# One chunk recurrence of a hybrid decoder layer: both head pairs of a batch in step, products in one array shape

## The chip, the core and the metric

The kernel runs on one core of a Trainium2 chip. The metric is the device time of one execution in microseconds (us). Engines are named as in the profile: PE is TensorE's matmul row and PEld its weight loads, DVE is VectorE, ACT ScalarE, POOL GpSimd, SP SyncE.

## What is computed

One layer over 256 tokens of width 2048: a wide input projection feeds three token mixers (Mamba-2 SSD, S5, RWKV-7), whose outputs are gated, merged, projected and normalised. The change touches the RWKV-7 mixer alone, 16 heads of 64:

```
def rwkv7_recurrence(r, w, k, v, a, bvec):
    b, s, h, n = r.shape

    def step(state, inp):
        r_t, w_t, k_t, v_t, a_t, b_t = inp
        sa = jnp.einsum('bhvk,bhk->bhv', state, a_t)
        state = (state * w_t[:, :, None, :] + sa[..., None] * b_t[:, :, None, :]
                 + v_t[..., None] * k_t[:, :, None, :])
        return state, jnp.einsum('bhvk,bhk->bhv', state, r_t)
...
    y = rwkv7_recurrence(rh, heads(decay), kh, vh, -kk, kk * heads(a))
    mean = jnp.mean(y, -1, keepdims=True)
    var = jnp.mean(jnp.square(y - mean), -1, keepdims=True)
    y = ((y - mean) * lax.rsqrt(var + RWKV_LNX_EPS)).reshape(b, s, RWKV_WIDTH) * lnx_w + lnx_b
```

The kernel does not step token by token. It cuts the 256 tokens into 4 chunks of 64 and writes each chunk as a few 64 by 64 products, with a triangular inverse for the part inside the chunk; only the state S goes from chunk to chunk.

## The kernel before

**Projections.** Most of the work is `proj`: a tile of 128 output columns, 16 blocks of the inner dimension, and for each block three matmuls of 128x128 by 128x256 in a reduced float32 format (L381 to L383), since weights and activations are split into a high and a low part. The weights come by DMA in half tiles (L367); ACT makes the high part (L369), DVE the low one (L371). Every half tile passes through a ring of four buffers.

**RWKV stage.** The 16 heads are 8 head pairs `hp` (a pair fills the 128 partitions, head 0 in rows 0 to 63, head 1 in rows 64 to 127); two pairs form a batch `b`, `i` is the pair in it. The list `PROG` gives the order of emission: `F` is the front of a batch, `T` the inverse of its diagonal blocks, `C` its chunk loop, the other entries are projections placed between. The framework's scheduler, which simulates a timeline, then sets each engine's order of instructions; each engine works through its own in order. So the small matmuls of the recurrence stand scattered between projections in PE's order, at most some twenty projections apart.

- `rwkv_prep` makes the operands of a head pair: `pv` (L585, V by token, four chunks of one head after the other), `pt` (L591, transposes of the stack of b and k), `pa` (L603, the products inside a chunk). `XS` holds the operands of the state product, `SVA` a stack of state and V for each head, `bkT` the transposed stacks, `MTr` the masked products with r.
- `rwkv_tinv` inverts the 32 by 32 diagonal blocks on DVE (L629, L630), brings them back by DMA into `TTf`, and adds the blocks beside the diagonal by three small products `py` (L647, L651, L655), 32 by 32.
- `rwkv_chunks` is the loop over four chunks, and in it over the two pairs of the batch. For each it multiplies XS by SVA (L675), copies the result to X (ACT, L677), multiplies by the inverse TTf (L680), copies it into SVA (ACT, L683), multiplies by bkT for the state's increment (L687), decays and adds the state (ACT L693, DVE L694; L690 in the first chunk), and forms the output: SVA by MTr (L697) plus, from the second chunk on, the old state by XS (L699). ACT copies the output to XS (L700). The next chunk begins with two ACT copies of S into SVA (L671).

These small products are in full float32, which PE does in two passes, each with its own weight load. L675 (but for the first chunk), L687 and L697 work on 128 rows and 64 columns of the array; L680, L699, L585 and the first chunk's L675 on 64 rows and 64 columns, one quadrant for each head.

Of the kernel before, what the change touches and what calls it, by code (L numbers as in the profile page):

```python
# [95 lines left out]
def pack(x, w_in, ssd_conv_w, ssd_conv_b, ssd_dt_bias, ssd_a_log, ssd_d, ssd_norm_w,  # L96
# [124 lines left out]
        # rings with one tile more than is alive, so that the low parts of a split take their sources' places  # L221
# [79 lines left out]
def setup(g):  # L301
# [3 lines left out]
    with tc.high_priority(), tc.tile_pool(name="xp", bufs=1) as xp:  # L305
# [11 lines left out]
        # step sizes of the SSD heads, kept in DRAM until their stage  # L317
# [28 lines left out]
    class Half:  # L346
        """[128, 16, 128] in two tiles of 8."""
# [59 lines left out]
CL = 64  # L407
# [3 lines left out]
def rwkv_setup(g):  # L411
# [10 lines left out]
    g.half = rp.tile([128, 2], F32, name="half")        # 0.5 | -0.5*exp(-0.5)  # L422
# [53 lines left out]
def rwkv_front(g, b):  # L476
# [13 lines left out]
    bt.XS, bt.bkT, bt.MTr, bt.SVA, bt.bon, bt.W4 = [], [], [], [], [], []  # L490
    bt.Aoff = rp.tile([128, 2, NCH, 32], F32, name=f"Aoff{b}", tag=f"Aoff{b % 2}", bufs=1)
    bt.TTf = rp.tile([128, 2, NCH, 64], F32, name=f"TTf{b}", tag=f"TTf{b % 2}", bufs=1)
    nc.gpsimd.memset(bt.TTf, 0.0)
    # blocks: [hp 2][c 4][h 2][half 2][s 32][t 32]
# [20 lines left out]
def rwkv_prep(g, bt, b, i, K, R, V, rh):  # L515
# [3 lines left out]
    # LoRA: decay logits and a logits  # L519
# [23 lines left out]
    W4 = rp.tile([128, NCH], F32, name=f"W4{hp}", tag="W4", bufs=4)  # L543
    nc.scalar.activation(W4, EE[:, :, CL], AF.Copy)
# [7 lines left out]
    # stack slots: 0 = head 0 (rows 0-63 A~, 64-127 Aak), 1 = head 1 (rows 0-63 Aak, 64-127 A~), 2 = r~  # L552
# [5 lines left out]
    # k2 = k*(1 + (a-1)*k_a); a = 0.5 + 0.5*tha  # L558
# [6 lines left out]
    BK = rp.tile([128, NCH, 3, CL], F32, name=f"BK{hp}", tag="BK", bufs=1)    # b, k, b  # L565
# [3 lines left out]
    # bonus = (sum r*k2*r_k) * v  # L569
# [6 lines left out]
    # token-major V, less its mean over the head (the recurrence is linear in V, so its outputs are centred), and (b, k) stacks  # L576
    SVA = rp.tile([128, 2, NCH, 64], F32, name=f"SVA{hp}", tag=f"SVA{b % 2}", bufs=2)
    bkT = rp.tile([128, 2, NCH, 64], F32, name=f"bkT{hp}", tag=f"bkT{b % 2}", bufs=2)
    pv = g.pp.tile([128, 2, NCH, 64], F32, name=f"pv{hp}", tag="s", bufs=2)
    idn = g.c("ident")  # L580
    for h in range(2):
        r = slice(64 * h, 64 * h + 64)
        o = slice(64 - 64 * h, 128 - 64 * h)
        for c in range(NCH):
            nc.tensor.matmul(pv[o, h, c, :], lhsT=V[r, CL * c:CL * c + CL], rhs=g.c("cen")[r, r], start=True, stop=True)  # L585
        nc.scalar.activation(SVA[o, h, :, :], pv[o, h, :, :], AF.Copy)
    for h in range(2):
        r = slice(64 * h, 64 * h + 64)
        pt = g.pp.tile([128, NCH, 64], F32, name=f"pt{hp}_{h}", tag="s", bufs=2)
        for c in range(NCH):  # L590
            nc.tensor.transpose(pt[:, c, :], BK[r, c, h:h + 2, :].rearrange("p a t -> p (a t)"), idn[r, r])  # L591
        nc.scalar.activation(bkT[:, h], pt, AF.Copy)
    # A stage
# [716 lines left out]
```

## Time and profile before

| | us |
|---|---|
| three runs | 1373.37, 1374.41, 1375.53 |
| median | 1374.41 |
| span of the profiled execution, first to last instruction | 1372.4 |
| PE busy in it | 1353.5 |
| DVE busy | 964.9 |
| ACT busy | 829.1 |

The profile holds the span of its execution and no other time of it; the median of the runs is 2.0 us above that span. In the views, a timeline row gives the start of an instruction and its duration; matmuls are pipelined, so that a row's duration reaches into the next rows, and the distance from start to start tells how fast PE goes. Rows of equal instructions that follow each other are merged, "x4" being four passes.

### The profile page before, as it was taken

The numbers are of one execution on the slowest core, as the hardware profiler recorded it, in microseconds if no ns is written. First come the engines' busy times: TensorE is split into PE (matmuls) and PEld (weight loads), VectorE is DVE, ScalarE is ACT, GpSimd is POOL, SyncE is SP. The second block draws the span as 40 slices with busy tenths as digits, with TensorE's granted clock in tenths as the row PEclk, the third lists the DMA queues.
The fourth block names the chain that finished last, engine by engine and source line by source line (L and its number), as shares of the span: only waits on it lengthen the run. The fifth ranks groups of instructions, "written<-read, shape, count | busy, mean of one in ns | idle before, by whom it ended". The sixth has DMA issues, their size and how long they took to land.

```text
span 1372.4 us, 28474 instructions
## 1 busy us (share of the span) xinstructions
PE 1353.5 (99%) x11436; PEld 1268.5 (92%) x11436; DVE 964.9 (70%) x1765; ACT 829.1 (60%) x1507; POOL 7.4 (1%) x54
## 2 busy tenths in 40 slices
PE   7999999999999999999999999999999999999996
PEld 7999989988999899899999999999999999999885
DVE  5658876455866765579999966799776665547755
ACT  5657565567555556887668877676645544444431
POOL 0000000000000000000000000000000000000000
PEclk9999999999999999999999999999999999999998
DMA  8545554433454345456555555555655556668751
GB/s 293 167 130 161 170 156 150 138 110 120 142 152 141 126 147 154 124 159 194 164 173 170 178 172 173 155 168 180 188 176 173 174 184 202 197 209 253 245 179 62
DMA packets 96661, 230.12 MB, mean 168 GB/s; under 512 B 26545, under 2 KB 41233, under 8 KB 96529
## 3 DMA queue, kind: packets, MB, share of 16 engines
q1 hardware_dynamic: 95936, 227.42, 53.9%
q8 instruction: 90, 1.47, 0.4%
q10 hardware_dynamic: 592, 0.89, 0.2%
q14 instruction: 43, 0.34, 0.1%
HBM read 224.00 MB, written 3.21 MB: 166 GB/s over the span
## 4 chain that ended last, share of the span: by engine, by line
PE 97%; ACT 1%; DMA 1%; DVE 1%; issue 0%; SPq 0%; DVEq 0%
PE ps_g L381 7%; PE ps_g L382 7%; PE ps_g L383 7%; PE ps_x L381 5%; PE ps_x L382 5%; PE ps_x L383 5%; PE br L1156 5%; PE br L1155 4%; PE br L1157 4%; PE po L1259 2%; PE po L1257 2%; PE po L1258 2%; PE ps_za L382 2%; PE ps_za L381 2%; PE ps_za L383 2%; PE ps_r L381 1%
## 5 line engine op out<-in xcount | busy, mean ns | idle before, releaser
L381 PE MATMUL ps_g<-xhi,hi_g 128*128 128x256 f32 x768 | 218.5, 284 | 0.0
L382 PE MATMUL ps_g<-xlo,hi_g 128*128 128x256 f32 x768 | 217.9, 284 | 0.0
L383 PE MATMUL ps_g<-xhi,lo_g 128*128 128x256 f32 x768 | 216.9, 282 | 0.0
L371 DVE TENSOR_TENSOR lo_g<-raw_g,hi_g 128x1024 fp32r<-128x1024 f32 x96 | 117.5, 1224 | 74.2 <-ACT hi_g L369 69.6
L369 ACT ACTIVATE hi_g<-raw_g 128x1024 fp32r<-128x1024 f32 x96 | 101.5, 1058 | 110.9 <-PE ps_g L382 81.8
L381 PE MATMUL ps_x<-xhi,hi_x 128*128 128x256 f32 x512 | 147.3, 288 | 0.0
L382 PE MATMUL ps_x<-xlo,hi_x 128*128 128x256 f32 x512 | 147.0, 287 | 0.0
L383 PE MATMUL ps_x<-xhi,lo_x 128*128 128x256 f32 x512 | 146.8, 287 | 0.0
L382 PEld LDWEIGHTS ps_g<-xlo,hi_g 128*128 128x128 f32 x768 | 144.6, 188 | 1.9 <-issue 0.8
L381 PEld LDWEIGHTS ps_g<-xhi,hi_g 128*128 128x128 f32 x768 | 144.6, 188 | 1.7
L383 PEld LDWEIGHTS ps_g<-xhi,lo_g 128*128 128x128 f32 x768 | 144.6, 188 | 0.9 <-issue 0.4
L369 ACT ACTIVATE hi_b<-raw_b 128x1024 fp32r<-128x1024 f32 x64 | 67.8, 1059 | 74.3 <-PE br L1156 42.9
L371 DVE TENSOR_TENSOR lo_x<-raw_x,hi_x 128x1024 fp32r<-128x1024 f32 x64 | 78.2, 1223 | 39.1 <-ACT hi_x L369 38.7
L381 PEld LDWEIGHTS ps_x<-xhi,hi_x 128*128 128x128 f32 x512 | 97.2, 190 | 2.3 <-issue 1.6
L382 PEld LDWEIGHTS ps_x<-xlo,hi_x 128*128 128x128 f32 x512 | 97.2, 190 | 2.1 <-issue 1.1
L383 PEld LDWEIGHTS ps_x<-xhi,lo_x 128*128 128x128 f32 x512 | 97.1, 190 | 1.6 <-issue 1.1
L369 ACT ACTIVATE hi_x<-raw_x 128x1024 fp32r<-128x1024 f32 x64 | 67.5, 1054 | 48.7 <-PE ps_x L382 25.1
L371 DVE TENSOR_TENSOR lo_b<-raw_b,hi_b 128x1024 fp32r<-128x1024 f32 x64 | 78.2, 1222 | 24.5 <-ACT hi_b L369 22.8
L382 PE MATMUL ps_za<-xlo,hi_za 128*128 128x256 f32 x256 | 73.1, 285 | 0.0
L381 PE MATMUL ps_za<-xhi,hi_za 128*128 128x256 f32 x256 | 73.0, 285 | 0.0
L383 PE MATMUL ps_za<-xhi,lo_za 128*128 128x256 f32 x256 | 72.6, 284 | 0.0
L1156 PE MATMUL br<-yh0l,hi_b 128*128 128x256 f32 x256 | 72.3, 283 | 0.0
(441 smaller groups left out, 4075.5 us busy)
## 6 DMA issues: line engine op xcount, KB each, us to landing
raw_g<-in_wt SPq DMA_DIRECT2D x96, 512.0 KB, 3.8
raw_x<-in_wt SPq DMA_DIRECT2D x64, 512.0 KB, 3.7
raw_za<-in_wt SPq DMA_DIRECT2D x32, 512.0 KB, 3.7
raw_b<-in_wba SPq DMA_DIRECT2D x32, 512.0 KB, 4.1
raw_wo<-in_wout SPq DMA_DIRECT2D x32, 512.0 KB, 4.7
raw_k<-in_wt SPq DMA_DIRECT2D x16, 512.0 KB, 3.8
raw_r<-in_wt SPq DMA_DIRECT2D x16, 512.0 KB, 3.7
raw_v<-in_wt SPq DMA_DIRECT2D x16, 512.0 KB, 3.6
```

Of the source, the lines that this page charges most:

```text
L369: nc.scalar.activation(hi, raw, AF.Copy)
L371: nc.vector.tensor_tensor(lo, raw, hi.bitcast(F32), ALU.subtract)
L381: nc.tensor.matmul(ps, lhsT=hi.k(k), rhs=g.xhi[:, k, :], start=(k == 0), stop=False)
L382: nc.tensor.matmul(ps, lhsT=hi.k(k), rhs=g.xlo[:, k, :], start=False, stop=False)
L383: nc.tensor.matmul(ps, lhsT=lo.k(k), rhs=g.xhi[:, k, :], start=False, stop=(k == NK - 1))
L1155: nc.tensor.matmul(ps, lhsT=hi.k(k0 + k), rhs=h, start=(k == 0), stop=False)
L1156: nc.tensor.matmul(ps, lhsT=hi.k(k0 + k), rhs=l, start=False, stop=False)
L1157: nc.tensor.matmul(ps, lhsT=lo.k(k0 + k), rhs=h, start=False, stop=(k == n - 1))
L1257: nc.tensor.matmul(po, lhsT=m[0][:, t], rhs=hi.k512(k), start=f0, stop=False)
L1258: nc.tensor.matmul(po, lhsT=m[0][:, t], rhs=lo.k512(k), start=False, stop=False)
L1259: nc.tensor.matmul(po, lhsT=m[1][:, t], rhs=hi.k512(k), start=False, stop=l0)
```

## The change

- In the chunk loop both pairs of a batch are done in step: one PSUM tile `ps` for both, one X copy, one copy into SVA for each head. The order of the matmuls is pair by pair with the two heads alternating.
- All five products of the loop use all 128 rows and 64 columns. Where an operand has only 64 rows of content, the others are zeros: `TTf` gets an axis for the head, the state is kept in `g.Sz` (two buffers, zeros in the other head's half), SVA's first chunk is zeroed.
- The state is written by DVE straight into SVA of the next chunk (add L710, multiply by the decay L711, for each head), and copied by ACT into `Sz` (L713). The fused operations L693, L694 and the copies L671 go.
- The output is gathered in a PSUM tile of its own, `chy`, for all four chunks, and copied once at the end; `ps` has two buffers instead of three.
- `pv` uses all 128 rows too, and in `pv`, `pt`, `pa` and the first product of `py` the loops run chunk by chunk with the heads alternating.

```
-            ps = g.pr.tile([128, 4, 64], F32, name=f"ch{hp}_{c}", tag="r", bufs=3)
+        ps = g.pr.tile([128, 3, 2, 64], F32, name=f"ch{b}_{c}", tag="r", bufs=2)
+        for i, h in IH:
+            nc.tensor.matmul(ps[rows[h], 0, i, :], lhsT=bt.XS[i][:, h, cs], rhs=SVA[:, i, h, c, :], start=True, stop=True)
+        X = rp.tile([128, 2, 64], F32, name=f"X{b}_{c}", tag="X", bufs=2)
+        nc.scalar.activation(X, ps[:, 0], AF.Copy)
+        for i, h in IH:
+            nc.tensor.matmul(ps[rows[h], 1, i, :], lhsT=bt.TTf[:, h, i, c, :], rhs=X[:, i, :], start=True, stop=True)
+        for h in range(2):
+            nc.scalar.activation(SVA[rows[h], :, h, c, :], ps[rows[h], 1], AF.Copy)
+        last = c == NCH - 1
+        if not last:
+            for i, h in IH:
+                nc.tensor.matmul(ps[rows[h], 2, i, :], lhsT=bt.bkT[i][:, h, c, :], rhs=SVA[:, i, h, c, :], start=True, stop=True)
...
+                nc.tensor.matmul(py[rows[h], i, cs], lhsT=SVA[:, i, h, c, :], rhs=bt.MTr[i][:, h, c, :], start=True, stop=(c == 0))
             for h in range(2):
...
+                if c > 0:
+                    nc.tensor.matmul(py[rows[h], i, cs], lhsT=Sz[:, i, h, :], rhs=bt.XS[i][:, 2, cs], start=False, stop=True)
+        if not last:
+            w = bt.W4[:, :, c:c + 1].to_broadcast([128, 2, 64])
+            Sn = g.Sz[c % 2]
...
+                    nc.vector.tensor_tensor(t, ps[r, 2], Sz[r, :, h, :], ALU.add)
+                    nc.vector.tensor_tensor(o, t, w[r], ALU.mult)
             for h in range(2):
...
+                nc.scalar.activation(Sn[rows[h], :, h, :], SVA[rows[h], :, h, c + 1, :], AF.Copy)
+            Sz = Sn
```

In `rwkv_prep`:

```
+    for c in range(NCH):
+        for h in range(2):
+            o = slice(64 - 64 * h, 128 - 64 * h)
+            nc.tensor.matmul(pv[o, h, c, :], lhsT=V[:, CL * c:CL * c + CL], rhs=g.c("cen")[:, 64 * h:64 * h + 64], start=True, stop=True)
...
+    pas = [g.pp.tile([128, NCH, 2, CL], F32, name=f"pa{hp}_{h}", tag="s", bufs=2) for h in range(2)]
+    for c in range(NCH):
+        for h in range(2):
+            r = slice(64 * h, 64 * h + 64)
+            rhs = XS[r, h:3:2 - h, CL * c:CL * c + CL]
+            nc.tensor.matmul(pas[h][:, c, :, :], lhsT=BK[r, c, h:h + 2, :].rearrange("p a t -> p (a t)"), rhs=rhs, start=True, stop=True)
```

What became of the order on PE, in batch 0. Before, at the outputs of the second chunk of pair 1 and the third of pair 0 (`ch1_1`, `ch0_2`), between the projections of a tile:

```order
L381 MATMUL ps_g2_5_3446<-xhi_69,hi_g2_5_1_3442 128x256
L697 MATMUL ch1_1_2083<-MTr1_877,SVA1_852 64x64
L699 MATMUL ch1_1_2083<-XS1_834,S1_0_2056 64x64
L697 MATMUL ch1_1_2083<-MTr1_877,SVA1_852 64x64
L699 MATMUL ch1_1_2083<-XS1_834,S1_0_2056 64x64
L697 MATMUL ch0_2_2105<-MTr0_649,SVA0_624 64x64
L699 MATMUL ch0_2_2105<-XS0_606,S0_1_2074 64x64
L697 MATMUL ch0_2_2105<-MTr0_649,SVA0_624 64x64
L699 MATMUL ch0_2_2105<-XS0_606,S0_1_2074 64x64
L675 MATMUL ch1_2_2127<-SVA1_852,XS1_834 64x64 x2
L382 MATMUL ps_g2_5_3446<-xlo_70,hi_g2_5_1_3442 128x256
```

And after, at the second chunk of batch 0 (L693 is now the product with bkT, L696 the one with MTr, L699 the one with the state):

```order
L382 MATMUL ps_g2_4_3246<-xlo_70,hi_g2_4_0_3236 128x256
L696 MATMUL chy0_2033<-MTr0_655,SVA0_448 64x64
L693 MATMUL ch0_1_2059<-SVA0_448,bkT0_631 64x64 x2
L693 MATMUL ch0_1_2059<-SVA0_448,bkT1_857 64x64 x2
L696 MATMUL chy0_2033<-MTr0_655,SVA0_448 64x64
L699 MATMUL chy0_2033<-XS0_613,Sz0_231 64x64 x2
L696 MATMUL chy0_2033<-MTr1_881,SVA0_448 64x64 x2
L699 MATMUL chy0_2033<-XS1_839,Sz0_231 64x64 x2
L383 MATMUL ps_g2_4_3246<-xhi_69,lo_g2_4_0_3238 128x256
```

The twelve matmuls of a chunk's end stand together in one shape (128 rows by 64 columns, all of them), where before the shape turned with every matmul.

On PE after the change, at `pt` of pair 0 and `pa` of pair 1 (the second number in `pa1_0` is the head); before, all of `pt` and `pa` stand in groups of one head:

```order
L601 MATMUL pt0_0_643<-cst_168,BK0_622 128x64 x4
L382 MATMUL ps_k2_918<-xlo_70,hi_k2_0_908 128x256
L383 MATMUL ps_k2_918<-xhi_69,lo_k2_0_910 128x256
L381 MATMUL ps_k2_918<-xhi_69,hi_k2_1_914 128x256
L382 MATMUL ps_k2_918<-xlo_70,hi_k2_1_914 128x256
L601 MATMUL pt0_1_644<-cst_168,BK0_622 128x64 x4
```

```order
L612 MATMUL pa1_0_882<-XS1_839,BK1_848 128x128 x2
L612 MATMUL pa1_1_883<-XS1_839,BK1_848 128x128 x2
L612 MATMUL pa1_0_882<-XS1_839,BK1_848 128x128
L612 MATMUL pa1_1_883<-XS1_839,BK1_848 128x128
L612 MATMUL pa1_0_882<-XS1_839,BK1_848 128x128
L612 MATMUL pa1_1_883<-XS1_839,BK1_848 128x128
```

The scheduler has put some of the alternating source back into groups of one head, and left some alternating.

On DVE after the change, at the state update of the second chunk of batch 0 (`St` is the sum, L371 are splits of projection weights, L641 and L642 belong to the inverse of batch 1):

```order
L641 TENSOR_TENSOR Pm1_2170<-TT1_2169,AT1_2168 128x256
L371 TENSOR_TENSOR lo_z4_1_3306<-raw_z4_1_3302,hi_z4_1_3304 128x1024
L642 TENSOR_REDUCE TT1_2169<-Pm1_2170 128x8
L710 TENSOR_TENSOR St0_1_2084<-ch0_1_2059,Sz0_231 64x128 x2
L711 TENSOR_TENSOR SVA0_448<-St0_1_2084,W40_447 64x2x64 x2
L371 TENSOR_TENSOR lo_g2_5_0_3364<-raw_g2_5_0_3360,hi_g2_5_0_3362 128x1024
```

Four operations stand where before there was one L694 for each pair, at two places.

## Rows read from the trace of the kernel before

**Rows 1.** The page, part 1: busy time, share of span, instructions.

```profile
PE 1353.5 (99%) x11436; PEld 1268.5 (92%) x11436; DVE 964.9 (70%) x1765; ACT 829.1 (60%) x1507; POOL 7.4 (1%) x54
```

**Rows 2.** All waits of PE: us in total, times, longest.

```profile
PE ps_dt L320 <- ACT wd L315: 7.0, 1, 7.0
PE ps_lora L383 <- DVE lo_lora L371: 0.4, 1, 0.4
```

**Rows 3.** Timeline of PE, 216.49 to 217.77: start, duration, engine, line, tiles.

```profile
216.49 0.28 PE L381 MATMUL ps_g<-xhi,hi_g 128*128 128x256 f32 x1
216.61 0.28 PE L382 MATMUL ps_g<-xlo,hi_g 128*128 128x256 f32 x1
216.82 0.33 PE L680 MATMUL ch<-X,TTf 64*64 64x64 f32 x2
217.08 0.39 PE L383 MATMUL ps_g<-xhi,lo_g 128*128 128x256 f32 x1
217.30 0.28 PE L381 MATMUL ps_g<-xhi,hi_g 128*128 128x256 f32 x1
217.51 0.34 PE L687 MATMUL ch<-SVA,bkT 128*64 128x64 f32 x4
217.77 0.39 PE L382 MATMUL ps_g<-xlo,hi_g 128*128 128x256 f32 x1
```

**Rows 4.** Timeline of PE at 198 us, first passes of two matmuls, different heads.

```profile
197.99 0.27 PE L680 MATMUL ch<-X,TTf 64*64 64x64 f32 x1
198.00 0.27 PE L675 MATMUL ch<-SVA,XS 64*64 64x64 f32 x1
```

**Rows 5.** Timeline of PE: eight passes of two heads in either shape.

```profile
228.68 0.45 PE L680 MATMUL ch<-X,TTf 64*64 64x64 f32 x8
229.06 0.39 PE L383 MATMUL ps_z<-xhi,lo_z 128*128 128x256 f32 x1
...
231.98 0.45 PE L687 MATMUL ch<-SVA,bkT 128*64 128x64 f32 x8
232.36 0.39 PE L382 MATMUL ps_g<-xlo,hi_g 128*128 128x256 f32 x1
```

**Rows 6.** Timeline of PE, 459.02 to 460.82: two shapes taking turns, eight times.

```profile
459.02 0.33 PE L697 MATMUL ch<-MTr,SVA 128*64 128x64 f32 x2
459.28 0.32 PE L699 MATMUL ch<-XS,S 64*64 64x64 f32 x2
...
460.82 0.33 PE L699 MATMUL ch<-XS,S 64*64 64x64 f32 x2
```

**Rows 7.** Timeline of PE: one head's `pv`, `py` of two heads, one head's `pa`.

```profile
117.86 0.68 PE L585 MATMUL pv<-cst,V 64*64 64x64 f32 x8
118.47 0.39 PE L383 MATMUL ps_z<-xhi,lo_z 128*128 128x256 f32 x1
...
176.16 0.69 PE L647 MATMUL py<-cst,TTf 32*32 32x32 f32 x16
176.78 0.33 PE L675 MATMUL ch<-SVA,XS 64*64 64x64 f32 x4
...
128.14 1.16 PE L603 MATMUL pa<-XS,BK 64*128 64x128 f32 x8
```

**Rows 8.** Window 462.00 to 465.20: busy PE, PEld, DVE, ACT, POOL; granted clock; DMA.

```profile
462.00:465.20 3.20, 3.20 (x17) 3.20 (x16) 2.40 (x6) 0.00 (x0) 0.00 (x0) 0.50 0.50 169
```

**Rows 9.** Groups by line: busy us, mean ns; idle before, releaser.

```profile
L369 ACT ACTIVATE hi_g<-raw_g 128x1024 fp32r<-128x1024 f32 x96 | 101.5, 1058 | 110.9 <-PE ps_g L382 81.8 <-issue 11.3 <-PE ps_u L382 5.5
L371 DVE TENSOR_TENSOR lo_g<-raw_g,hi_g 128x1024 fp32r<-128x1024 f32 x96 | 117.5, 1224 | 74.2 <-ACT hi_g L369 69.6 <-PE s5pk L1064 4.2
L694 DVE SCALAR_TENSOR_TENSOR S<-ch,W,SW 128x64 f32<-128x64 f32 x16 | 4.2, 274 | 12.1 <-PE ch L687 10.8 <-ACT SVA L683 1.2
```

**Rows 10.** Weight loads of L697: four in the timeline; all, with the mean ns.

```profile
205.13 0.20 PEld L697 LDWEIGHTS ch<-MTr,SVA 128*64 128x64 f32 x4
...
L697 PEld LDWEIGHTS ch<-MTr,SVA 128*64 128x64 f32 x128 | 11.1, 135 | 5.3
```

More of the change, by code (lines that the diff above doesn't have):

```diff
@@ L432, in rwkv_setup @@
     g.rhl = [rhl[64 * q:64 * q + 64, :] for q in range(2)]
+    g.Sz = [rp.tile([128, 2, 2, 64], F32, name=f"Sz{q}") for q in range(2)]
+    for q in range(2):
+        nc.gpsimd.memset(g.Sz[q], 0.0)
     g.selT = [selT[64 * q:64 * q + 64] for q in range(2)]
@@ L489, in rwkv_front @@
     bt = Ctx()
[L490 removed]
+    bt.XS, bt.bkT, bt.MTr, bt.bon = [], [], [], []
     bt.Aoff = rp.tile([128, 2, NCH, 32], F32, name=f"Aoff{b}", tag=f"Aoff{b % 2}", bufs=1)
[L492 removed]
+    bt.TTf = rp.tile([128, 2, 2, NCH, 64], F32, name=f"TTf{b}", tag=f"TTf{b % 2}", bufs=1)
+    bt.W4 = rp.tile([128, 2, NCH], F32, name=f"W4{b}", tag=f"W4{b % 2}", bufs=1)
+    bt.SVA = rp.tile([128, 2, 2, NCH, 64], F32, name=f"SVA{b}", tag=f"SVA{b % 2}", bufs=1)
+    for h in range(2):
+        nc.gpsimd.memset(bt.SVA[64 * h:64 * h + 64, :, h, 0, :], 0.0)
     nc.gpsimd.memset(bt.TTf, 0.0)
@@ L575, in rwkv_prep @@
     nc.vector.tensor_tensor(bon, pb, V, ALU.mult)
-    SVA = rp.tile([128, 2, NCH, 64], F32, name=f"SVA{hp}", tag=f"SVA{b % 2}", bufs=2)
+    SVA = bt.SVA
     bkT = rp.tile([128, 2, NCH, 64], F32, name=f"bkT{hp}", tag=f"bkT{b % 2}", bufs=2)
@@ L586, in rwkv_prep @@
-        nc.scalar.activation(SVA[o, h, :, :], pv[o, h, :, :], AF.Copy)
-    for h in range(2):
[L588 to L592, printed above, removed]
+        nc.scalar.activation(SVA[o, i, h, :, :], pv[o, h, :, :], AF.Copy)
+    pt = [g.pp.tile([128, NCH, 64], F32, name=f"pt{hp}_{h}", tag="s", bufs=2) for h in range(2)]
@@ L596, in rwkv_prep @@
+    for c in range(NCH):
+        for h in range(2):
+            r = slice(64 * h, 64 * h + 64)
+            rhs = XS[r, h:3:2 - h, CL * c:CL * c + CL]
+            nc.tensor.matmul(pas[h][:, c, :, :], lhsT=BK[r, c, h:h + 2, :].rearrange("p a t -> p (a t)"), rhs=rhs, start=True, stop=True)
     for h in range(2):
-        r = slice(64 * h, 64 * h + 64)
         o = slice(64 - 64 * h, 128 - 64 * h)
-        pa = g.pp.tile([128, NCH, 2, CL], F32, name=f"pa{hp}_{h}", tag="s", bufs=2)
-        for c in range(NCH):
-            cs = slice(CL * c, CL * c + CL)
-            rhs = XS[r, h:3:2 - h, cs]
-            nc.tensor.matmul(pa[:, c, :, :], lhsT=BK[r, c, h:h + 2, :].rearrange("p a t -> p (a t)"), rhs=rhs, start=True, stop=True)
+        pa = pas[h]
@@ L641, in rwkv_tinv @@
     for i in range(2):
-        py = g.pr.tile([128, 3, NCH, 32], F32, name=f"py{b}_{i}", tag="r", bufs=3)
+        py = g.pr.tile([128, 3, NCH, 32], F32, name=f"py{b}_{i}", tag="r", bufs=2)
         Y = rp.tile([128, 2, NCH, 32], F32, name=f"Yl{b}_{i}", tag="Yl", bufs=1)
         hs = [(slice(64 * h, 64 * h + 32), slice(64 * h + 32, 64 * h + 64)) for h in range(2)]
+        for c in range(NCH):
+            for h, (lo, hi) in enumerate(hs):
+                nc.tensor.matmul(py[lo, 0, c, :], lhsT=bt.TTf[lo, h, i, c, 0:32], rhs=idn[lo, lo], start=True, stop=True)
         for lo, hi in hs:
-            for c in range(NCH):
-                nc.tensor.matmul(py[lo, 0, c, :], lhsT=bt.TTf[lo, i, c, 0:32], rhs=idn[lo, lo], start=True, stop=True)
             nc.scalar.activation(Y[lo, 0], py[lo, 0], AF.Copy)
@@ L652, in rwkv_tinv @@
             nc.scalar.activation(Y[hi, 1], py[hi, 1], AF.Copy)
-        for lo, hi in hs:
+        for h, (lo, hi) in enumerate(hs):
             for c in range(NCH):
-                nc.tensor.matmul(py[lo, 2, c, :], lhsT=Y[hi, 1, c, :], rhs=bt.TTf[hi, i, c, 32:64], start=True, stop=True)
-            nc.scalar.activation(bt.TTf[lo, i, :, 32:64], py[lo, 2], AF.Copy)
+                nc.tensor.matmul(py[lo, 2, c, :], lhsT=Y[hi, 1, c, :], rhs=bt.TTf[hi, h, i, c, 32:64], start=True, stop=True)
+            nc.scalar.activation(bt.TTf[lo, h, i, :, 32:64], py[lo, 2], AF.Copy)
@@ L659, in rwkv_chunks @@
 def rwkv_chunks(g, bt, b):
     nc, rp = g.nc, g.rp
[L661 removed]
+    SVA, IH = bt.SVA, [(i, h) for i in range(2) for h in range(2)]
+    rows = [slice(64 * h, 64 * h + 64) for h in range(2)]
+    py = g.pr.tile([128, 2, T], F32, name=f"chy{b}", tag="y", bufs=1)
+    Sz = None
     for c in range(NCH):
         cs = slice(CL * c, CL * c + CL)
[L664 to L688 removed]
@@ L689, in rwkv_chunks @@
+        if not last:
+            w = bt.W4[:, :, c:c + 1].to_broadcast([128, 2, 64])
+            Sn = g.Sz[c % 2]
+            St = rp.tile([128, 2, 64], F32, name=f"St{b}_{c}", tag="St") if c > 0 else None
+            for h in range(2):
+                r, o = rows[h], SVA[rows[h], :, h, c + 1, :]
                 if c == 0:
-                    nc.vector.tensor_scalar(Sn, ps[:, 2, :], W4[:, c:c + 1], None, ALU.mult)
+                    nc.vector.tensor_tensor(o, ps[r, 2], w[r], ALU.mult)
@@ L697, in rwkv_chunks @@
-                nc.tensor.matmul(ps[r, 3, :], lhsT=SVA[:, h, c, :], rhs=MTr[:, h, c, :], start=True, stop=(c == 0))
-                if c > 0:
-                    nc.tensor.matmul(ps[r, 3, :], lhsT=S[i][r, :], rhs=XS[r, 2, cs], start=False, stop=True)
-            nc.scalar.activation(XS[:, 2, cs], ps[:, 3, :], AF.Copy)
-            if c < NCH - 1:
-                S[i] = Sn
-    sqs = []
+                nc.scalar.activation(Sn[rows[h], :, h, :], SVA[rows[h], :, h, c + 1, :], AF.Copy)
+            Sz = Sn
```

52 lines of the change are left out of this document (14 added, 38 removed).

## Prediction

> **What bounds the kernel now.** I read the page's busy shares first, then TensorE's waits, then the start times of single matmuls. TensorE (PE) is marked busy 1353.5 of 1372.4 us [rows 1], and it waits for another engine only twice in the whole program, 7.0 us at the start and 0.4 us [rows 2]. So the time is the sum of the distances between the starts of its matmuls, and the reader should look at those distances, not at the durations, since matmuls overlap. Projections follow each other every 0.12 us [rows 3]. When the array's shape changes, the distance grows: from a projection to a small matmul 0.21 us; after two passes of one head the next projection starts 0.26 us later; the projection after that only 0.22 us later instead of 0.12 [rows 3]. (A float32 matmul is two passes, so the x2 in a row is one matmul.) The same visit with both heads, x4, also takes 0.26 us [rows 3]: the second head is nearly free, because it sits on other columns or another quadrant of the array and starts 0.01 us after the first [rows 4]. A run of eight passes, two heads by four, takes 0.38 us [rows 5], so each further pair of passes costs (0.38 - 0.26) / 2 = 0.06 us, or 0.12 us for a pair of matmuls. But when the next small matmul has another shape, the whole 0.26 us is paid again for each single matmul [rows 6]. The recurrence of before is full of that: L697 has 128 rows by 64 columns, L699 has 64 by 64, and they take turns head by head.
>
> **What the change costs and saves, on PE.** No matmul is added or dropped, only shapes and order change; I counted runs in the order of the built programs, and priced them with the rows.
>
> Chunk products (L675, L680, L687, L697, L699; 288 matmuls in both programs). Before they make 188 runs of one shape with 53 further steps in them: 188 x 0.26 + 53 x 0.06 = 52.1 us. After they begin 59 runs with 211 further steps: 59 x 0.26 + 211 x 0.06 = 28.0, and 0.4 for the few that ride in a run of another product: 28.4. That is **-23.7 us**. Padding 64 rows to 128 costs nothing on PE: eight passes take 0.38 us at 64x64 as at 128x64 [rows 5].
>
> V's transposes `pv`: 8 passes of one head take 0.61 us [rows 7]. Before there are 16 such runs, after 8, in which the other head's passes lie beside them: **-4.9 us**.
>
> `py`, first product: 16 passes one behind the other take 0.62 us with leaving [rows 7], about 0.031 each once 0.12 for leaving is taken off. 128 passes become about 64 steps: 2.0, and a little for fewer runs, **-2.2 us**.
>
> `pa` (and `pt`): the source alternates heads, but the order does this only in part. Of the eight head pairs, three still stand four by four with projections between, three start two by two, and two alternate throughout. Eight passes of `pa` take 1.16 us less the last one's own 0.28, about 0.12 each [rows 7]. By the order some 28 of 128 passes get cover: **-3 us**, between 0 (if halves of the rows don't overlap at this width) and -7 (everything alternating).
>
> Visits: the projections' shape is left 203 times before and 193 times after, each at 0.09 on entry and 0.10 on the second projection back [rows 3]: **-1.9 us**.
>
> Sum on PE: -35.7 us.
>
> Clock. Once, right after 2 us of nothing but turns of L697 and L699 [rows 6], the granted clock fell to 0.50, the lower level of 1.2 GHz, for 3.2 us: 17 projections at about 0.2 us instead of 0.12, so 1.4 us lost [rows 8]. After the change the recurrence has no visit of even 1.5 us by these prices, so I take **-1.4 us**; it may stay (0).
>
> Other engines. ScalarE loses some hundred small copies (L671, L693 and L700 of before go; wider ones and two copies of the state come). VectorE gets two adds and two multiplies a chunk (L710, L711) for two fused operations (L694). Both are off the path: no row of PE's waits names them but for those two [rows 2]. GpSimd gets memsets of the padding, issued a batch ahead. What could cost is a new wait: PE's queue is in order, so if a copy or the state update comes late, all projections behind it stand. There are 44 hand-offs (16 of X, 16 of SVA, 12 of the state), and the order puts 20 to 30 projections ahead of nearly all, at least 2.4 us. A copy of some 0.3 us behind one weight split of ScalarE, 1.06 us, fits [rows 9]. The state update isn't in the trace of before; its nearest row is L694 at 0.27 us, so four operations are 1.1 us, behind one weight split of VectorE of 1.22 us 2.3 us [rows 9], just covered; behind two splits it is 1.1 us late, twelve times 13 us. Queued behind L710 are the splits of the next projection's weights, needed a tile (48 projections, 5.7 us) later. I take **+1 us**, nearest to the row of PE's waits, with 0 and 13 as the ends. PSUM's `r` goes from three buffers to two; as one now holds both pairs, the same number of steps is in flight.
>
> Total: -35.7 - 1.4 + 1 = -36.1 us. The span becomes 1372.4 - 36.1 = 1336.3. The median of the three runs, 1374.4, lies 2.0 above that span, which I keep: **1338 us**.
>
> **One rule that speaks against this.** The row shows that four weight loads of L697, both heads, take 0.20 us together where one alone takes 0.135, so the loads of two heads with the same 128 rows do overlap [rows 10]. The Trainium skill, page "TensorE: Matmul & The Clock Gate", section "Part 3: Packing small matmuls — row/col tiling", says that a weight load overlaps running matmuls only when the row groups differ. By that rule padding every operand to all rows would take the overlap away; the trace disagrees, and I follow the row.
>
> **Rivals.** (1) Heads on the same rows don't overlap over long runs. Then the chunk products take 59 x 0.26 and one step for each further pass, 42 us in all instead of 28; `pv`, `py` and `pa` keep their old time, 10 us: +24, about **1362 us**. Against it: the x4 and x8 runs at 128x64 [rows 3, 5]. (2) Waits take part of the gain: 13 us by the bound above, or more where ScalarE's queue is long, 8 to 30 us, so **1346 to 1368 us**. For it: the pairs now march in step, so that one pair's products no longer fill the other's waits. Against: 2.4 us of projections stand in each gap, and PE never waited before with the same cover. (3) Slower than before, by the same hand-offs: 36 us over 44 of them is 0.8 us each on top of the cover, so it decides from hand-offs of about 3.3 us, three weight splits ahead of each copy. At 1.2 us over, 53 us are lost: **1391 us**. The order has one split, seldom two, between such copies. (4) The change doesn't do what it says: already true of `pt` and `pa`; if the paired order were lost in the chunk products too, with shapes alike but heads one behind the other, the time is that of (1).
>
> **How the numbers follow.** Forecast (1331 to 1346) 0.80; rival 2 0.09; rival 1 and 4 0.05; better than 1331 0.02; slower 0.02; within the measurement 0.02, where half of rival 3 happens. About 0.2% (2.7 us) is what a measurement of this kernel can tell from no change. So faster 0.96, same 0.02, slower 0.02. The range: the sum's bounds give 1333 (all of `pa` covered, no wait) to 1355 (`pa` nothing, clock fall kept, 13 us of waits); I cut the top at 1350, since these seldom come together, and put the bottom at 1331, since the prices are rounded to 0.01 us.
>
> **What would show it.** In the changed profile: no 64x64 matmuls in the recurrence; runs of L696, L693 and L699 of 12 matmuls in about 0.9 us where before each single matmul took 0.26; L593 x16 in about 0.6 us; PE's waits still without VectorE and ScalarE after the first 20 us; the stage up to the last chunk some 36 us shorter, everything behind it as long as before; no fall of the clock in the recurrence. Wrong if L710 or L685 turn up among PE's releasers with more than some us, or if x4 runs at 128x64 take 0.37 instead of 0.26 us.

## The result and the profile after

The changed kernel takes **1344.03 us** (median of four runs, 1342.44 to 1345.58), the kernel before 1374.97 in the same comparison; the ratio is 0.9775, with a 95% interval of 0.9762 to 0.9789. Forecast were 1338 us and a range of 1331 to 1350. The profiled execution has a span of 1340.7 us where 1336.3 were forecast: -31.7 us in place of -36.1.

The page of the changed kernel, its span and part 1 (compare [rows 1]):

```profile
span 1340.7 us, 28364 instructions
PE 1316.9 (98%) x11436; PEld 1242.3 (93%) x11436; DVE 970.9 (72%) x1781; ACT 809.9 (60%) x1392; POOL 11.3 (1%) x64
```

PE still sets the time, with the same 11436 passes. All its waits (us in total, times, longest), which answer to [rows 2]:

```profile
PE ps_dt L320 <- ACT wd L315: 7.2, 1, 7.2
PE s5pk L1076 <- ACT s5WT L1072: 3.0, 1, 3.0
PE py L659 <- DMA TTf<-Td: 0.7, 1, 0.7
PE y L868 <- ACT ST L847: 0.7, 1, 0.7
PE nb L892 <- ACT dg L890: 0.5, 1, 0.5
PE ps_dt L321 <- DVE xlo L312: 0.2, 1, 0.2
```

Two rows have become six: 12.3 us instead of 7.4. None of the new ones is a hand-off of the chunk loop (L685, L689 and L710 don't appear), and the largest of the new ones, 3.0 us, is in the first S5 tile, which the change doesn't touch.

Timeline of PE in the changed kernel: a run of `pv`, the start of a chunk and the end of one, each with the projection behind it (start, duration, engine, line, tiles; they answer to [rows 3 to 7]):

```profile
108.63 0.69 PE L593 MATMUL pv<-cst,V 128*64 128x64 f32 x16
109.25 0.39 PE L383 MATMUL ps_z<-xhi,lo_z 128*128 128x256 f32 x1
...
207.79 0.45 PE L683 MATMUL ch<-SVA,XS 128*64 128x64 f32 x8
208.17 0.39 PE L381 MATMUL ps_g<-xhi,hi_g 128*128 128x256 f32 x1
...
214.16 0.27 PE L696 MATMUL chy<-MTr,SVA 128*64 128x64 f32 x1
...
214.79 0.34 PE L699 MATMUL chy<-XS,Sz 128*64 128x64 f32 x4
215.05 0.39 PE L383 MATMUL ps_g<-xhi,lo_g 128*128 128x256 f32 x1
```

The chunk end holds twelve matmuls, 24 passes, and lasts from 214.16 to 215.05, 0.89 us; in [rows 6] each single matmul took 0.26. L683 takes 0.38 us for two heads and two pairs, as the prediction read from [rows 5]; sixteen passes of `pv` take 0.62 us, where eight took 0.61 [rows 7].

Adding, in the trace, the distances from each matmul's start to the next one's start gives what each product occupies of PE (a wait ahead of a product counts to the one before it):

| | before | after | difference | forecast |
|---|---|---|---|---|
| five chunk products | 51.2 | 26.9 | -24.3 | -23.7 |
| `pv` | 9.7 | 4.8 | -4.9 | -4.9 |
| `py`, first product | 5.2 | 3.1 | -2.1 | -2.2 |
| `pa` and `pt` | 21.0 | 16.8 | -4.2 | -3 |
| `py`, second and third | 11.7 | 11.6 | -0.1 | 0 |
| waits of PE | 7.4 | 12.3 | +4.9 | +1 |

The products come to -35.6 and the waits to +4.9. The projections' shape is left 193 times instead of 203, as the order said; what the projections' distances hold beyond 0.119 us each, waits and slow stretches left out, falls from 40.7 to 38.8 us, so -1.9, the prediction's price. That is -32.6 against the span's -31.7; the distance from the first to the last matmul, without the wait ahead of the first, shrank by 31.9 (1353.8 to 1321.9).

The clock fall of [rows 8] has not gone but moved. Two windows of the changed kernel, the wait in the S5 tile and the stretch behind it (columns as in [rows 8]):

```profile
596.13:599.72 3.59, 0.63 (x6) 0.40 (x6) 3.59 (x8) 3.51 (x7) 0.10 (x1) 1.00 0.36 136
600.40:603.60 3.20, 3.08 (x18) 2.81 (x17) 2.64 (x11) 3.10 (x10) 0.11 (x1) 0.50 0.61 171
```

PE works 0.63 of 3.59 us, and behind it the granted clock is at the lower level, 1.2 GHz, for as long as it was in the kernel before (3.4 us by the clock's records in both).

### The profile page after: what moved, and what is told of

Same layout as the page of the kernel before. It is cut to its first block, busy times and chain, and to the rows that moved or that the text cites. A ratio compares the mean times of both kernels' runs of the same rounds, so it can differ in the third digit from the quotient of the medians.

```text
span 1340.7 us, 28364 instructions
## 1 busy us (share of the span) xinstructions
PE 1316.9 (98%) x11436; PEld 1242.3 (93%) x11436; DVE 970.9 (72%) x1781; ACT 809.9 (60%) x1392; POOL 11.3 (1%) x64
## 4 chain that ended last, share of the span: by engine, by line
PE 96%; ACT 2%; DMA 1%; DVE 1%; issue 0%; SPq 0%; DVEq 0%; ACTq 0%
PE ps_g L381 7%; PE ps_g L382 7%; PE ps_g L383 7%; PE br L1169 5%; PE br L1168 5%; PE br L1167 5%; PE ps_x L381 4%; PE ps_x L383 4%; PE ps_x L382 4%; PE ps_za L381 2%; PE po L1271 2%; PE po L1270 2%; PE po L1269 2%; PE ps_za L383 2%; PE ps_za L382 2%; PE ps_r L381 1%
## 5 line engine op out<-in xcount | busy, mean ns | idle before, releaser
L381 PE MATMUL ps_g<-xhi,hi_g 128*128 128x256 f32 x768 | 218.1, 284 | 0.0
L371 DVE TENSOR_TENSOR lo_g<-raw_g,hi_g 128x1024 fp32r<-128x1024 f32 x96 | 117.4, 1223 | 74.4 <-ACT hi_g L369 69.2
L381 PEld LDWEIGHTS ps_g<-xhi,hi_g 128*128 128x128 f32 x768 | 144.6, 188 | 2.2 <-issue 1.1
L381 PE MATMUL ps_x<-xhi,hi_x 128*128 128x256 f32 x512 | 146.2, 286 | 0.0
L371 DVE TENSOR_TENSOR lo_x<-raw_x,hi_x 128x1024 fp32r<-128x1024 f32 x64 | 78.2, 1221 | 32.6 <-ACT hi_x L369 32.6
L381 PEld LDWEIGHTS ps_x<-xhi,hi_x 128*128 128x128 f32 x512 | 96.5, 188 | 2.2 <-issue 1.6
L371 DVE TENSOR_TENSOR lo_b<-raw_b,hi_b 128x1024 fp32r<-128x1024 f32 x64 | 78.2, 1222 | 25.9 <-ACT hi_b L369 23.9
L381 PE MATMUL ps_za<-xhi,hi_za 128*128 128x256 f32 x256 | 73.4, 287 | 0.0
```

The costliest lines, as they stand in the source:

```text
L371: nc.vector.tensor_tensor(lo, raw, hi.bitcast(F32), ALU.subtract)
L381: nc.tensor.matmul(ps, lhsT=hi.k(k), rhs=g.xhi[:, k, :], start=(k == 0), stop=False)
```

## The wait that was not in the sum

Timeline of ACT in the changed kernel, the queue ahead of the copy that PE waits for:

```profile
596.63 0.55 ACT L802 ACTIVATE C<-ps_x,par 128x256 f32<-128x256 f32 x1
...
597.62 1.28 ACT L886 ACT_TABLE_LOAD   x1
598.92 0.26 ACT L886 ACTIVATE rs<-nr,ssdeps 128x2 f32<-128x2 f32 x1
599.08 0.59 ACT L1072 ACTIVATE s5WT<-s5pb 128x512 f32<-128x512 f32 x1
```

And of PE over the same time:

```profile
596.13 0.63 PE L1070 MATMUL s5pb<-cst,s5W 128*128 128x128 f32 x4
599.72 0.33 PE L1076 MATMUL s5pk<-s5cq,s5W 128*32 128x32 f32 x16 [2.96 <-ACT s5WT L1072]
```

The four transposes `s5pb` end at 596.76; their copy comes behind five other things in ACT's queue (two S5 rows left out), a table load of 1.28 us among them. `s5pk` shares the PSUM buffer, so it waits. In the kernel before the same tile is at 662 us, and 26 projections of the branches stand in PE's order between the last transpose and `s5pk`:

```profile
662.48 0.49 PE L1058 MATMUL s5pb<-cst,s5W 128*128 128x128 f32 x3
...
665.80 0.28 PE L1157 MATMUL br<-ych,lo_b 128*128 128x256 f32 x1
666.01 0.33 PE L1064 MATMUL s5pk<-s5cq,s5W 128*32 128x32 f32 x16
```

In the changed kernel no projection stands there. The recurrence is over sooner (the last chunk product starts at 522 instead of 585 us, since the scheduler also packs it more tightly), and the scheduler put the S5 tile into another place, ahead of the branches.

## Experiments

Ratios are to the kernel before on the same chip; the changed kernel has 0.9775. One per cent is 13.7 us.

**Heads apart.** The changed kernel with

```
-    SVA, IH = bt.SVA, [(i, h) for i in range(2) for h in range(2)]
+    SVA, IH = bt.SVA, [(i, h) for h in range(2) for i in range(2)]
...
-        for i in range(2):
-            for h in range(2):
-                nc.tensor.matmul(py[rows[h], i, cs], lhsT=SVA[:, i, h, c, :], ...)
...
+        for i, h in IH:
+            nc.tensor.matmul(py[rows[h], i, cs], lhsT=SVA[:, i, h, c, :], ...)
...
```

> The changed kernel with one thing taken back: inside a chunk the products keep one array shape (128x64, padded operands) and both pairs stay in step, but each pass over the four (pair, head) blocks goes head 0, head 0, head 1, head 1, where the changed kernel goes head 0, head 1, head 0, head 1. Theory (two column tiles of the same shape overlap although they use the same 128 rows, so a product pays only where two neighbours share a column tile): the products of the chunks, 29.6 us in the changed kernel when start-to-start times of the trace are added up in the built order, become 38.5 us, the time about 1352 us (+8). [...]

Measured 1348.74 us, ratio 0.9818 (0.9805 to 0.9832): about 6 us slower than the changed kernel by the ratios, 5.6 from first to last matmul in the trace, of which the chunk products make 5.0 (26.9 to 31.9, summed as in the table above; the expectation's 29.6 comes from another sum, over the built order). PE's timeline of the same chunk end as above:

```profile
214.57 0.33 PE L695 MATMUL chy<-MTr,SVA 128*64 128x64 f32 x2
214.74 0.45 PE L693 MATMUL ch<-SVA,bkT 128*64 128x64 f32 x8
...
215.49 0.28 PE L697 MATMUL chy<-XS,Sz 128*64 128x64 f32 x2
215.70 0.39 PE L382 MATMUL ps_g<-xlo,hi_g 128*128 128x256 f32 x1
```

1.13 us instead of 0.89. If two heads on the same 128 rows did not overlap, their order could not matter. It has a price, so tiles of the same rows and other columns do overlap, and rival (1) falls. But the price is little over half of what I expected; the last two experiments say why.

**Two shapes again.** The changed kernel with

```
-            nc.tensor.matmul(ps[rows[h], 1, i, :], lhsT=bt.TTf[:, h, i, c, :], rhs=X[:, i, :], ...)
+            nc.tensor.matmul(ps[rows[h], 1, i, :], lhsT=bt.TTf[rows[h], h, i, c, :], rhs=X[rows[h], i, :], ...)
...
-                    nc.tensor.matmul(py[rows[h], i, cs], lhsT=Sz[:, i, h, :], rhs=bt.XS[i][:, 2, cs], ...)
+                    nc.tensor.matmul(py[rows[h], i, cs], lhsT=Sz[rows[h], i, h, :], rhs=bt.XS[i][rows[h], 2, cs], ...)
```

> The changed kernel with one thing taken back: the product with TTf and the one with the state read 64 rows again (64x64, no padding), so that each chunk changes the array shape four times; both pairs still in step and heads still alternating. Theory (a turn of the shape costs about 0.15 us that no neighbour covers): 462 against 423 stretches of one shape in the built order, some 39 turns more at 0.15 us, +5.7 us, about 1350 us. Rival (padding costs as much as it saves, since 128 rows have to be loaded in place of 64): no difference or up to 3 us faster, 1341 to 1344 us.

Measured 1350.25 us, ratio 0.9826 (0.9812 to 0.9841), 7 us slower than the changed kernel by the ratios. In the trace the chunk products rise from 26.9 to 32.1, and that at the places where the shapes meet: L696 by 3.4, L699 by 1.9. The product with TTf, which stands alone in its run, doesn't move (7.7 and 7.6): padding is free. The chunk end in PE's timeline:

```profile
216.19 0.27 PE L696 MATMUL chy<-MTr,SVA 128*64 128x64 f32 x1
...
216.74 0.33 PE L699 MATMUL chy<-XS,Sz 64*64 64x64 f32 x4
217.00 0.34 PE L696 MATMUL chy<-MTr,SVA 128*64 128x64 f32 x4
217.26 0.33 PE L699 MATMUL chy<-XS,Sz 64*64 64x64 f32 x4
217.53 0.39 PE L383 MATMUL ps_g<-xhi,lo_g 128*128 128x256 f32 x1
```

1.34 us where one shape takes 0.89: three turns more, 0.15 each. The trace is 7.7 us longer from first to last matmul. Beside the 5.2 of the chunk products stand 1.6 us more of waits and a second stretch of half clock (about 1.4 us by the prediction's price); together they come near the rest, but no run takes them apart.

**Fronts as before.** The changed kernel with `pv`, `pt`, `pa` and the first product of `py` taken back, for example

```
-    for c in range(NCH):
-        for h in range(2):
-            o = slice(64 - 64 * h, 128 - 64 * h)
-            nc.tensor.matmul(pv[o, h, c, :], lhsT=V[:, CL * c:CL * c + CL], rhs=g.c("cen")[:, 64 * h:64 * h + 64], ...)
     for h in range(2):
+        r = slice(64 * h, 64 * h + 64)
         o = slice(64 - 64 * h, 128 - 64 * h)
+        for c in range(NCH):
+            nc.tensor.matmul(pv[o, h, c, :], lhsT=V[r, CL * c:CL * c + CL], rhs=g.c("cen")[r, r], ...)
```

> The changed kernel with the work ahead of the chunks taken back to that of the kernel before: pv unpadded on 64 rows, and pv, pt, pa and the first product of py head by head. Prediction's terms for these edits: 4.9 for pv, 2.2 for py, 3 for pa and pt, together 10.1 us; start-to-start times added up in the built order give 14.0. So about 1354 to 1358 us. Here the order on ScalarE puts the copy L1072 of the first S5 tile elsewhere, and the 3.0 us wait of the changed kernel may be absent, which would take up to 3 us off: 1351 to 1358. Rival (all the gain is in the chunks): 1344 us.

Measured 1351.77 us, ratio 0.9837 (0.9823 to 0.985), 8.5 us slower by the ratios and 8.7 in the trace. The four products rise by 11.9 (`pv` 5.0, `pa` 3.8, `py` 2.3, `pt` 0.9), and here the S5 tile stands among projections again (24 between the transposes and `s5pk`), so that its wait is absent. The largest waits of PE in this kernel:

```profile
PE ps_dt L320 <- ACT wd L315: 7.1, 1, 7.1
PE y L859 <- ACT ST L842: 1.2, 1, 1.2
```

No slow stretch stands behind it either. So the fronts are worth some 12 us in their products, and the changed kernel kept 8.5 of them.

**One shape alone.** The kernel before with all operands of the chunk loop padded, pairs still one after the other (the state's tiles also share two tags where there were four, a second difference that is not tested apart):

```
-                nc.tensor.matmul(ps[r, 1, :], lhsT=bt.TTf[r, i, c, :], rhs=X[r, :], ...)
+                nc.tensor.matmul(ps[r, 1, :], lhsT=bt.TTf[:, h, i, c, :], rhs=X, ...)
...
+                    nc.scalar.activation(g.Sz[i][r, h, :], S[i][r, :], AF.Copy)
...
-                    nc.tensor.matmul(ps[r, 3, :], lhsT=S[i][r, :], rhs=XS[r, 2, cs], ...)
+                    nc.tensor.matmul(ps[r, 3, :], lhsT=g.Sz[i][:, h, :], rhs=XS[:, 2, cs], ...)
```

> The kernel before with one part of the change alone: all products of a chunk in the shape 128x64 with padded operands (a padded copy of the state is made by one more ScalarE copy for each head and chunk); the pairs of a batch still one after the other, the work ahead of the chunks as before. Theory (turns of the array shape are what costs, whatever the order of the pairs): start-to-start times of the trace added up in the built order give 14.9 us less than before, 1360 us (ratio 0.989), so more than half of what the chunks gained. If the model overstates here as it did for the heads apart (8.1 forecast, 4.7 measured), some 9 to 15: 1360 to 1366. Rival (only the two pairs in step bring the gain, since one pair alone has too few independent products to fill the array, or the added copies are on the path from state to state): 1372 to 1375 us.

Measured 1363.62 us, ratio 0.9921 (0.9908 to 0.9935): 11 us faster than before. The chunk products fall from 51.2 to 33.6; doing the pairs in step takes them on to 26.9. So one shape makes 17.6 of the 24.3, the rest of the loop's change, pairs in step above all, 6.7. Not all of the 17.6 arrives; among PE's waits of this kernel are new ones,

```profile
PE y L859 <- ACT ST L842: 1.6, 1, 1.6
PE ch L704 <- ACT SVA L690: 1.0, 1, 1.0
PE y L859 <- DVE csb L853: 0.9, 1, 0.9
```

(11.1 us of waits in all, 3.7 more than before), and the clock is low for 6.8 us instead of 3.4, another 1.4 by the prediction's price. The visits take 1.3 us more (41.9 instead of 40.7, read as above). Less than 1 us is left that I cannot place.

**Fronts alone.** The kernel before with the fronts of the changed one (the edit of the one before last, the other way round).

> The kernel before with the other part alone: pv padded and alternating, pt, pa and the first product of py alternating between the heads; the chunks as before. Theory: the lines of these products lose what they lost in the changed kernel (12.3 us between the changed kernel and the one with the fronts taken back), less what the scheduler undoes; the built order gives 9.1. So 1363 to 1366 us (ratio 0.991 to 0.993). Rival (part of it is taken back by a wait at a place where TensorE comes early, as at the first S5 tile in the changed kernel, up to 4.5 us): 1367 to 1370 us.

Measured 1370.09 us, ratio 0.9969 (0.9958 to 0.9981): 4.3 us faster, which is the far end of the rival's range. The four products do lose 9.0 in the trace (`pv` 4.5, `pa` 2.6, `py` 1.6, `pt` 0.3). Against it stand 3.3 us more of waits,

```profile
PE s5pk L1068 <- ACT s5WT L1064: 1.5, 1, 1.5
PE py L650 <- DMA TTf<-Td: 1.3, 1, 1.3
```

among them, and the product with TTf rises by 1.6; the projections `ps_k` among the fronts are broken off for another shape 18 times instead of 7, and the visits in all take 1.3 us more (42.0 instead of 40.7). The scheduler's new order gave back more than half, for the clock fall of the kernel before is absent here too.

**One table load less.** The changed kernel without the square root of one SSD group, and so without the table load ahead of it:

```
-    nc.scalar.activation(rs, p5, AF.Sqrt, scale=1.0 / 256, bias=g.ssdeps)
+    nc.scalar.activation(rs, p5, AF.Identity if gr == 2 else AF.Sqrt, scale=1.0 / 256, bias=g.ssdeps)
```

> The changed kernel with TensorE's order the same row for row, and one ScalarE table load (1.28 us) and the load that turns the table back less: in SSD group 2 the square root of L886 is left out (the function is Identity there), so that group's norm is wrong. The load stands ahead of the copy L1072 that TensorE waits 3.0 us for. Theory (that wait is on the path to the end and is made by ScalarE's queue): the wait becomes 1.7 us, the time 1342.7 us (-1.3). Second theory (the clock's fall to 0.50 behind the wait is made by the wait): with 1.7 us of wait the fall may be gone as well, another 1.5 us, 1341.2 us. Rival (the loss is given back by a later wait, since other work is what ends last): 1344 us.

Measured 1342.69 us, ratio 0.9773 (0.976 to 0.9787), not to be told from the changed kernel; the span is 1340.6 against 1340.7. Its waits of PE:

```profile
PE s5pk L1076 <- ACT s5WT L1072: 1.5, 1, 1.5
PE py L659 <- DMA TTf<-Td: 1.3, 1, 1.3
```

The wait halved, as expected, so ACT's queue makes it. But laid beside the changed kernel's, row by row (PE's order is the same), the matmuls are 1.0 us late from 167 us on, behind a longer wait for the inverse's DMA; 0.5 early after the S5 wait; and level again at 604 us. The low clock begins 0.7 us later (601.0 instead of 600.3) and lasts 3.4 us as before, but in this kernel it falls on projections from its start, where the first 1.2 us of it held S5's small products: 14 distances of 0.21 us between projections instead of nine. The windows of this kernel (the granted clock is the third number from the end; in the changed kernel they show 0.50 and 0.99):

```profile
600.30:603.70 3.40, 3.09 (x14) 3.01 (x15) 3.40 (x15) 2.99 (x12) 0.07 (x1) 0.60 0.80 192
603.70:606.00 2.30, 2.30 (x18) 2.25 (x16) 2.30 (x10) 1.78 (x9) 0.03 (x1) 0.85 0.64 236
```

So half the wait is no saving by itself here, and the slow stretch doesn't need a wait of 3 us.

**S5 copy first.** The same, with the S5 operand, its transposes and the copy L1072 also raised in the scheduler:

```
+    with g.tc.high_priority():
         pb = g.ps.tile([128, 2, 2, 128], F32, name=f"s5pb{i}", tag="r", bufs=1)
...
         A.activation(WT, pb, AF.Copy)
```

> The changed kernel with the first S5 operand, its transposes and their copy given priority, and in SSD group 2 the square root of L886 left out (Identity in its place, no table load), so that group's norm is wrong. The copy then stands directly behind L802 and L886 on ScalarE. With the table load alone left out the wait went from 3.0 to 1.5 us but the stretch at half clock stayed (3.4 us of it). Theory: the wait goes to 1.0 us or less; if the slow stretch comes from TensorE's idle time here it is now gone too, and the time is 1340 us (2 us of wait and 1.5 us of slow clock); if the slow stretch stays, 1342 us. Rival (neither is on the path): 1344 us.

Measured 1342.37 us, ratio 0.9768 (0.9754 to 0.9781). The wait split up instead of going to 1.0:

```profile
597.78 0.71 PE L1108 MATMUL s5bu<-s5U,s5WT 64*128 64x128 f32 x8 [1.11 <-ACT s5WT L1074]
...
599.77 0.69 PE L1130 MATMUL s5y<-yb,s5k 128*128 128x128 f32 x2 [1.02 <-ACT s5k L1082]
```

2.1 us instead of 3.0, the slow stretch still there (from 599.9 us), 1.6 us gained from first to last matmul. The tile is a chain over ACT and back; pulling one link forward leaves the next to wait. What covers it is other work on PE.

**All of `py` alternating.** The changed kernel with

```
-        for lo, hi in hs:
-            for c in range(NCH):
+        for c in range(NCH):
+            for lo, hi in hs:
                 nc.tensor.matmul(py[hi, 1, c, :], lhsT=bt.Aoff[lo, i, c, :], rhs=Y[lo, 0, c, :], ...)
```

and the same for the third product.

> The changed kernel and one step more: the second and third product of py also go head 0, head 1 in each chunk's turn, in place of one head after the other. The first product lost 2.1 us of 5.2 that way; the two together take 11.6 us, so 4.2 to 5.7 us less. By the built order the first S5 tile's transposes, copy and products stand between products of the branches, so the 3.0 us wait and the slow stretch behind it should be absent. Theory (that wait and the slow stretch cost the changed kernel 4.5 us, which the recurrence had already gained): 1334 to 1335.5 us. Rival (the wait costs nothing, as it is idle time that would come elsewhere): 1338 to 1340 us. Second rival (the alternation brings nothing since the products wait for ScalarE's copies between them): 1339.5 without the wait, 1344 with it.

Measured **1328.80 us**, ratio 0.9669 (0.9656 to 0.9682), the best of all and better than expected. PE's timeline, first in this kernel and then in the changed one:

```profile
171.81 0.44 PE L664 MATMUL py<-Yl,Aoff 32*32 32x32 f32 x16
172.18 0.39 PE L382 MATMUL ps_r<-xlo,hi_r 128*128 128x256 f32 x1
```

```profile
170.28 0.43 PE L664 MATMUL py<-Yl,Aoff 32*32 32x32 f32 x8
170.65 0.38 PE L382 MATMUL ps_r<-xlo,hi_r 128*128 128x256 f32 x1
```

Sixteen passes take 0.37 us, as eight did. The two products lose 5.7 us (11.6 to 5.9), `pa` and the product with TTf 1.5, and the S5 tile has 40 matmuls between transposes and `s5pk`: the 3.0 us there are gone, though 1.4 come in a wait at L381. The array's shape turns 392 times instead of 423, the projections' is left 177 times instead of 193. A slow stretch is there, early in the program now. The visits fall by another 3.9 us, read as above (38.8 to 34.8). In the trace all this is 12.7 us, by the ratios 14.6. The expectation left the visits out, and in the trace they are about what it was short of; no run takes them apart from the rest.

**Two by two.** This best kernel with head 0, head 0, head 1, head 1 in the second and third product of `py`:

```
-        for c in range(NCH):
-            for lo, hi in hs:
-                nc.tensor.matmul(py[hi, 1, c, :], ...)
+        for c, (lo, hi) in [(c0 + d, p) for c0 in (0, 2) for p in hs for d in range(2)]:
+            nc.tensor.matmul(py[hi, 1, c, :], ...)
```

> The kernel with all of py alternating, changed in one thing: the second and third product go head 0, head 0, head 1, head 1 in place of head 0, head 1, head 0, head 1. Theory A (one product of a head may stand in front and the other head's product still starts: with the heads apart in the chunks, eight passes of the product with XS took 0.39 us against 0.38): a run of 16 passes still takes 0.37 us, the lines of the two products together 6.0 us as before, time 1329 us. Theory B (strictly in order: the second product of a head waits for the first, and the other head's behind it): runs of 16 passes take longer, about 0.47, together 1.6 us more, 1330 to 1331 us. The trace's rows tell, the time alone doesn't.

Measured 1331.21 us, ratio 0.9693 (0.9674 to 0.9712); the trace decides:

```profile
170.59 0.46 PE L663 MATMUL py<-Yl,Aoff 32*32 32x32 f32 x16
170.98 0.38 PE L382 MATMUL ps_r<-xlo,hi_r 128*128 128x256 f32 x1
```

0.39 us instead of 0.37, 0.3 us in the whole program: theory A.

**Heads apart, but not in the outputs.** The changed kernel with the first of the two edits of "heads apart" alone.

> The changed kernel with the heads apart (head 0, head 0, head 1, head 1) in the products with XS, TTf and bkT alone, the output products in the order of the changed kernel. Theory A (two of a head in a row cost nothing, three do): XS and TTf keep 7.0 and 7.7 us, and only the runs in which the product with bkT stands behind one with MTr of the same head, three of head 0 in a row, pay, up to 0.1 us in each of 12, 1.2 us: 1344 to 1345.5 us. Theory B (strictly in order): every run of these products pays, by the sums in the built order 6.2 us: 1350 us.

Measured 1347.6 us, ratio 0.9807 (0.979 to 0.9825). Here neither theory gives the size. The chunk products take 29.8 instead of 26.9, +2.9, and the waits for the inverse's DMA 2.3 instead of 0.7; a second slow stretch is there as well. Of the 2.9, L693 and L696 make 1.6, as theory A had it. The product with XS makes 1.1, and the rows show where; first this kernel, then the changed one:

```profile
388.97 0.45 PE L683 MATMUL ch<-SVA,XS 128*64 128x64 f32 x4
389.34 0.43 PE L664 MATMUL py<-Yl,Aoff 32*32 32x32 f32 x8
```

```profile
385.92 0.34 PE L683 MATMUL ch<-SVA,XS 128*64 128x64 f32 x4
386.18 0.43 PE L664 MATMUL py<-Yl,Aoff 32*32 32x32 f32 x8
```

In a run of two matmuls both are of one head now, 0.37 us instead of 0.26. Runs of four matmuls take 0.39 against 0.38.

## Why the prediction was right, and where it was not

**What bounds it.** Right: PE's order and the distances between starts. Every term of the sum that is made of them came within 1.2 us, most within 0.6; `pa` and `pt` gave 4.2 for 3, the visits 1.9 as forecast. The experiments bear out the two mechanisms apart: turns of the shape (17.6 us of the chunk products by one shape alone, 5.2 lost again with two shapes), and heads side by side (5.0 lost with the heads apart, and the fronts' 12 us).

**Padding is free.** Right: the product with TTf takes 7.7 us at 128x64 and 7.6 at 64x64, in two kernels whose loops differ in the operands' shapes alone.

**The rule against it.** The Trainium skill, page "TensorE: Matmul & The Clock Gate", section "Part 3: Packing small matmuls — row/col tiling", lets a weight load overlap running matmuls only where the row groups differ. The runs don't bear it out for tiles of other columns: 0.26 us for one matmul each of two heads on the same 128 rows, 0.37 us for two of one head (last experiment). Rows 10, on which the prediction went, were a weak ground for it: in that place the second pass's load also starts 0.055 us after the first's, which takes 0.133, so that loads of one head overlap each other as well. The starts of the matmuls are what shows it.

**The waits.** This term failed. I gave +1 us, with 13 as the far end, and looked for it in the chunk loop's 44 hand-offs. It measured +4.9 us, none of it there; 3.0 are in an S5 tile that the diff doesn't touch. Nor did the sign hold that PE's waits would be without ACT after the first 20 us. The step that failed is "PE never waited before with the same cover": the cover is not the same, because work behind the recurrence moves too when the scheduler plans anew. The order of the changed kernel, which I had, shows `s5pb` and `s5pk` side by side; I read only the places that the diff names. "Everything behind it as long as before" was wrong for the same reason, and the end of the last chunk was a bad thing to watch: it came 63 us earlier, with a gain of 32.

**The clock.** Also wrong: -1.4 became 0. There is no fall in the recurrence now, but one of the same length stands behind the S5 wait. Beside the one at the very end, which all kernels have and which the prediction's "once" passed over, most have such a stretch in one place or another; three have none (the fronts taken back, the fronts alone, two by two), and two have two. What sets it off is not settled by these runs: with the wait ahead of it halved it was still there, 0.7 us later.

Taken together: forecast -36.1, of which the waits (3.9 more) and the clock (1.4 more) take back 5.3, and the products, `pa` and the chunk products above all, add 1.8: -32.6. The span shrank by 31.7; some 0.9 us I cannot place. So part of the nearness to the forecast is luck: products that gained more than forecast covered a third of what the waits and the clock took back.

**Rivals.** (1) is excluded by the heads apart. (2) is what happened, in size below its own range and at another place. (3), slower by the hand-offs, had nothing for it: no hand-off of the chunk loop shows in PE's waits. (4) is true of part of `pt` and `pa`, as said.

## What to carry to other kernels

Where an engine is bound by its own order, count the runs of one array shape and price a run by its first pair and each further step: that gave every term of this change that is made of distances to within 1.2 us. Pad small operands to the shape of their neighbours, and let at most two products of one tile stand in a row before the other tile's follow in the same run. And read the new order at all places where the engine has little else to do, not only at the edited ones: the gain that went missing was lost to a chain over another engine that had been covered before.

## What the runs showed of the hardware

A tile need not alternate strictly. With head 0, head 0, head 1, head 1, eight passes of the product with XS take 0.39 us against 0.38, and sixteen of `py` 0.39 against 0.37. The trace of the heads apart has the eight in one row:

```profile
219.81 0.46 PE L683 MATMUL ch<-SVA,XS 128*64 128x64 f32 x8
220.20 0.39 PE L382 MATMUL ps_g<-xlo,hi_g 128*128 128x256 f32 x1
```

Pass by pass the starts come in pairs, 219.809 and 219.823, 219.916 and 219.929. A row doesn't name its head; but two first passes of 0.270 us stand at the front, where a head alone has one and its second pass 0.107 us later (at 388.97 in the last experiment). So I take the second of each pair as the other head's: its first pass starts 0.014 us after the first, though a whole matmul of head 0 stands between them in the order. With three of one head in a row it doesn't: at 214.57 two passes of L695 run alone for 0.17 us before the other head starts, 214.74. And four in a row, as in `py` of the changed kernel, get nothing: 0.37 us for eight passes, as long as sixteen of both heads alternating.
